# Projections two chunks at a time, latent statistics and key rope moved, attention's products in another order, in a two-layer hybrid decoder trunk on one NeuronCore

## The chip, the core and the metric

The kernel runs on one core of a Trainium2 chip. The metric is the device time of one execution in microseconds (us). TensorE (PE) multiplies, VectorE (DVE) and ScalarE (ACT) do the element-wise work, SyncE (SP) issues nearly all DMAs. TensorE writes to eight PSUM banks of 128 x 512 fp32.

## The reference

```python
# x: 256 tokens x 2048; layer 0: short convolution, layer 1: latent attention; both with a squared-ReLU MLP
bcu = h @ w_in                                   # 2048 -> 6144
gate_b, gate_c, u = split(bcu, 3)
mix = (gate_b * causal_conv3(gate_c * u)) @ w_out
h = LN(ALPHA * h + mix)
h = LN(ALPHA * h + square(relu(h @ w1)) @ w2)    # 2048 -> 8192 -> 2048
# layer 1
ckv = h @ w_dkv                                  # 512 latents and 64 for the key rope
c, k_pe = rms_norm(ckv[:, :512]) , rope(ckv[:, 512:])
k, v = split_heads(c @ w_ukv)                    # 16 heads, 128 each
q, q_pe = split_heads(rms_norm(h @ w_dq) @ w_uq) # 128 and 64 a head
p = softmax(mask((q @ k.T + rope(q_pe) @ k_pe.T) * 192 ** -0.5))
mix = (p @ v) @ w_o
h = LN(ALPHA * h + mix)
h = LN(ALPHA * h + square(relu(h @ w1)) @ w2)
```

## The kernel before

All products keep fp32 accuracy with a faster format: each fp32 operand is split into a high part (`hi`, ScalarE's cast) and a low part (`lo`, VectorE's subtraction). Activations stand transposed, high and low side by side in 512 columns, so a weight tile's high part meets 512 columns and its low part 256.

Weights come as units of 128 x 1024 (two for a chunk of 128 output columns from 2048 inputs). `stream` lists them in order of use; `take(n)` hands out the next n and has `make_up_to` load and split further ones ahead. The ring of finished parts has `WA = 8` slots, that of raw loads `RAW = 6`. Tiles in PSUM come from `psum`: four banks (`pmm`), and four more while `Banks` is open, which is so except in attention and in the parallel stretches of the MLP.

The order of the instructions on each engine is that of the code, changed by the framework's scheduler where dependencies allow; in the MLPs a planner (`Work`) writes it out.

The stages: an opening that multiplies while the first rows arrive, the input projection (`products(3 * NC, xhl, begun)`, 48 chunks in the order c, u, b, with the convolution between), the output projection (`products(NC, z)`, 16 chunks, name `ps_u` in both), the first MLP, the latents, attention, its output projection (three chunks in `out_first`, named `ps_wo`, then `products(NC - WO_G, oT)`, 13), the second MLP.

`mm_like` multiplies one chunk: 16 matmuls on high parts, then 16 on low parts. `products` takes a chunk, multiplies it and yields its bank.

At the first MLP's end `down` adds the last partial products into four blocks of 512 outputs, and `turned(n)` transposes a block into four chunks of 128 outputs (names `turned`, `xres`), which `summed` adds to the residual, counts for the layer norm (`S`, `Q`) and multiplies by the gain for the next product (`xd`). The next products are the latents: `group_of(GROUP)` opens three chunks (`ps_g`), which `mm_wide` runs over the inputs that are there.

The latents are nine chunks (four for keys and values, one for the key rope, four for queries); from the fourth on they are named `ps_w`. `latent` normalises a chunk after the fact, splits it and adds its squares (`csq`, `qsq`). `rms` turns those into a factor by a matmul with a column (`rstat`) and a root on a few values: `rc` for keys and values, spread over a tile `rk` by `spread` (`rkp`), and `rq`, from which `query_scale` makes `sc` and `nsc`. `rope` takes a product by cosines and four or two products by sines of 32 rows each, and a sum.

Attention runs in groups of four heads. `project(g)` makes a group's keys (`ps_k`, cleared by VectorE with `rk`), queries (`ps_q`, cleared by ScalarE), values (`ps_v`, ScalarE) and query ropes (`ps_p`, VectorE's `rope`), and yields after each; between its yields stands one step of `attention(g - 1)`: scores `S`, softmax, transposes `tp`, and the product with the values `po`. Only the four banks of `pmm` are left for `project`; attention has four of its own.

Of the kernel before, what the change touches and what calls it, by code (L numbers as in the profile page):

```python
# [53 lines left out]
def trunk(ctx: ExitStack, tc: tile.TileContext, opening, xT, vecs, w_in, w_out, w_kv, w_q, w_uk, w_uv,  # L54
# [75 lines left out]
    stream += mlp_stream(0)  # L130
    stream += mlp_end(0) + halves(w_kv) + halves(w_q)
    for g in range(4):
        stream += halves(w_uk[g]) + halves(w_qn[g]) + halves(w_uv[g]) + halves(w_qp[g])
    stream += halves(w_o) + mlp_stream(1)
    stream += mlp_end(1)
    size = {"unit": 1, "plain": 2}
# [108 lines left out]
            high(ps, w, k, x[k], k == 0)  # L245
            low(ps, w, k, x[k], k == nk - 1)

    def mm_like(ps, w, x, n=NC):

        for h in range(0, NC, n):  # L250
            for k in range(h, h + n):
                high(ps, w, k, x[k], k == 0)
            for k in range(h, h + n):
                low(ps, w, k, x[k], k == NC - 1)

    def mm_k1(ps, w, blk, x, first, last):
# [24 lines left out]
    def products(n, x, begun=()):  # L281

        yield from begun
        for i in range(len(begun), n):
            w = take()
            ps = psum("ps_u")
            mm_like(ps, w, x)
            yield ps


    def dot(ps, w, x, first, last, goes_on=False):
# [84 lines left out]
    class Norm:  # L376
# [10 lines left out]
        def means(self):  # L387

            ps = psum("mu0c")
            for t in range(2):  # L390
                tensor.matmul(ps[:, t:t + 1], xres[:, 0, t * P:(t + 1) * P], ones[:, 0:1], start=True, stop=True)
            self.off = small.tile([P, 2], F32, tag="off", name="off", bufs=1)
            vector.tensor_scalar(self.off, ps[:, 0:2], -self.scale, None, ALU.mult)

        def prepare(self, m):
# [690 lines left out]

    def to_wide(block, put, h):

        def turned(n):
            for c in range(2):  # L1090
                ps = psum("turned")
                for j in range(4):
                    src = block(n, j % 2)[:, (2 * c + j // 2) * P:(2 * c + j // 2 + 1) * P]
                    tensor.transpose(ps[:, j * P:(j + 1) * P], src, id_t)
                summed(ln, [ps[:, j * T:(j + 1) * T] for j in range(2)], scaled, 4 * n + 2 * c)

        ln.widen("b")
        for n in range(NB):
            down(h, put, n)
            if n:  # L1100
                turned(n - 1)
        ln.ws = group_of(GROUP)
        mm_wide(ln.ws, ln.xd, 0, NC - 4)
        turned(NB - 1)
        mm_wide(ln.ws, ln.xd, NC - 4)

    before, ln = ln, Norm(1, ALPHA)
# [6 lines left out]
    with tc.tile_pool(name="att", bufs=1) as ap:  # L1114
# [60 lines left out]
        pss = wide_products()  # L1175
        for m in range(NK):
            latent(next(pss), m, chl, C_KG, csq)
        f = tmp.tile([P, T], F32, tag="fh", name="fpe", bufs=3)
        ln.weighted(next(pss), f)
        for j in range(2):  # L1180
            rope(kpe[:, j, :], f, slice(64 * j, 64 * j + 64))
        for m in range(NK):
            ps = next(pss)
            if m == 0:
                rms(rc, csq)
            if m == 2:
                rkp = psum("rkp")
                spread(rkp, rc)
                scalar.copy(rk, rkp[:, :T])
            latent(ps, m, qhl, C_QG, qsq)  # L1190
        rq = small.tile([P, 2], F32, tag="rr", name="rq")

        def query_scale():
# [13 lines left out]
        with tc.tile_pool(name="att2", bufs=2) as a2, \  # L1207
                tc.tile_pool(name="paux", bufs=1, space=PS) as paux:
            def project(g, box):

                k4, q4, p4, v4 = (t[g % 2] for t in (k2, q2, p2, v2))
                box.update(k=k4, q=q4, p=p4, v=v4)
                w = take()
                for j in range(4):
                    ps = psum("ps_k")
                    mm(ps, w, 4 * j, chl, NK)
                    vector.tensor_tensor(k4[:, j, :], ps[:, :T], rk, ALU.mult)
                    yield
                w = take()
                for j in range(4):  # L1220
                    ps = psum("ps_q")
                    mm(ps, w, 4 * j, qhl, NK)
                    scalar.copy(q4[:, j, :], ps[:, :T])
                    yield
                if g == 0:
                    query_scale()
                for _ in range(2):
                    ln.normal(next(todo))
                w = take()
                for b in range(2):  # L1230
                    ps = psum("ps_v")
                    for k in range(NK):
                        dot(ps, wide_rows(w[k // 2], k % 2), held(chl[k], b), k == 0, k == NK - 1)
                    scalar.activation(v4[:, b, :], ps, AF.Copy, scale=rc[:, b:b + 1])
                    yield
                w = take(1)
                for j in range(2):
                    ps = psum("ps_p")
                    mm(ps, w, 4 * j, qhl, NK)
                    rope(p4[:, j, :], ps[:, :T], slice(0, P))  # L1240
                    yield

            def attend(h, box):

                j = h % 4
                qn, kn = box["q"][:, j, :], box["k"][:, j, :]
                qp, kp = box["p"][:, j // 2, :], kpe[:, h % 2, :]
                S = paux.tile([P, 512], F32, tag="S", name=f"S_{h}", bufs=2)
                spans = ((0, P), (P, T))
                for b, (at, n) in enumerate(spans):  # L1250
                    tok = slice(b * P, (b + 1) * P)
                    tensor.matmul(S[:, at:at + n], qn[:, tok], kn[:, :n], start=True, stop=False)
                    tensor.matmul(S[:, at:at + n], qp[:, tok], kp[:, :n], start=False, stop=True)
                pr = pr2[h % 2]
                mx = small.tile([P, 2], F32, tag="mx", name="mx")
                su = small.tile([P, 2], F32, tag="su", name="su")
                vector.tensor_tensor(pr, S[:, :3 * P], mask_t, ALU.add)
                for b, (at, n) in enumerate(spans):
                    vector.tensor_reduce(mx[:, b:b + 1], pr[:, at:at + n], AX.X, ALU.max)
                vector.tensor_tensor(mx, mx, nsc, ALU.mult)  # L1260
                for b, (at, n) in enumerate(spans):
                    scalar.activation(pr[:, at:at + n], pr[:, at:at + n], AF.Exp, bias=mx[:, b:b + 1],
                                         scale=sc[:, b:b + 1], accum_out=su[:, b:b + 1])
                vector.reciprocal(su, su)
                for b, (at, n) in enumerate(spans):
                    vector.tensor_scalar(pr[:, at:at + n], pr[:, at:at + n], su[:, b:b + 1], None, ALU.mult)
                yield
                tp = paux.tile([P, 512], F32, tag="ta", name="tp")
                for n in range(3):
                    tensor.transpose(tp[:, n * P:(n + 1) * P], pr[:, n * P:(n + 1) * P], id_t)  # L1270
                pt = a2.tile([P, 3 * P], F32, tag="pt", name=f"pt_{h}")
                scalar.copy(pt, tp[:, :3 * P])
                yield
                po = paux.tile([P, 512], F32, tag="tb", name="po")
                vv = box["v"]
                tensor.matmul(po[:, :T], vv[:, 0, j * P:(j + 1) * P], pt[:, :T], start=True, stop=False)
                tensor.matmul(po[:, P:T], vv[:, 1, j * P:(j + 1) * P], pt[:, T:], start=False, stop=True)
                put_split(oT[h], po[:, :T])
                yield

            def attention(g, box):
                gens = [attend(4 * g + j, box) for j in range(4)]
                for step in range(6):
                    for j in range(3, -1, -1):
                        if 0 <= step - j < 3:
                            next(gens[j])
                            yield

            first_o = []
            after = Norm(2, ALPHA)  # L1290

            def out_first():

                for i in range(WO_G):
                    first_o.append((take(), psum("ps_wo")))
                for k in range(H):
                    mm_run(first_o, oT, k, k + 1, H)
                    after.prepare(k)
                    yield

            prev = None
            for g in range(5):
                box = {}
                a = attention(g - 1, prev) if prev is not None else iter(())
                b = project(g, box) if g < 4 else out_first()
                done_a = done_b = False
                while not (done_a and done_b):
                    done_a = next(a, 0) == 0
                    done_b = next(b, 0) == 0
                prev = box  # L1310
# [143 lines left out]
```

## Time and profile before

| | us |
|---|---|
| median of 3 runs | 1997.64 |
| lowest and highest | 1997.62, 1998.24 |
| the profiled execution | 1998.73 |
| its span, first to last instruction | 1996.9 |

| stage, us from the span's start | PE busy | DVE busy | ACT busy |
|---|---|---|---|
| 100 to 150, input projection | 50.00 | 32.08 | 23.09 |
| 300 to 350, output projection | 50.00 | 39.04 | 25.31 |
| 500 to 600, first MLP | 100.00 | 95.97 | 85.50 |
| 1050 to 1100, latents | 48.62 | 44.71 | 34.73 |
| 1100 to 1150, latents and attention | 49.63 | 42.55 | 33.16 |
| 1250 to 1300, attention's output projection | 50.00 | 39.56 | 25.30 |

Nearly every instruction is recorded by one helper and so has line L71: groups are told apart by their names, `out<-in`. A row of the timeline has start, length, engine, line, operation, names, shape and count, and in square brackets the idle time before and what ended it. A matmul's end is modelled, and records of neighbours overlap: their pace is read from the starts.

### The profile page before, as it was taken

The numbers are of one execution on the slowest core, as the hardware profiler recorded it, in microseconds if no ns is written. First come the engines' busy times: TensorE is split into PE (matmuls) and PEld (weight loads), VectorE is DVE, ScalarE is ACT, GpSimd is POOL, SyncE is SP. The second block draws the span as 40 slices with busy tenths as digits, with TensorE's granted clock in tenths as the row PEclk, the third lists the DMA queues.
The fourth block names the chain that finished last, engine by engine and source line by source line (L and its number), as shares of the span: only waits on it lengthen the run. The fifth ranks groups of instructions, "written<-read, shape, count | busy, mean of one in ns | idle before, by whom it ended". The sixth has DMA issues, their size and how long they took to land.

```text
span 1996.9 us, 29770 instructions
## 1 busy us (share of the span) xinstructions
PE 1983.1 (99%) x11058; PEld 1735.0 (87%) x11058; DVE 1752.6 (88%) x2630; ACT 1388.6 (70%) x2069; POOL 2.3 (0%) x21
## 2 busy tenths in 40 slices
PE   9999999999999999999999999999999999999997
PEld 8888888988888888888889998898888888888886
DVE  7667667689999999999988888878999999999997
ACT  6444445577887888878856655567788788887871
POOL 0000000000000000000000000000000000000000
PEclk9999999999999999999999999999999999999999
DMA  9755556456666666666765543644666666666673
GB/s 341 230 188 189 191 186 188 156 164 195 208 200 202 205 202 205 200 202 207 221 208 158 165 129 117 204 163 154 201 203 206 200 203 204 202 206 202 199 248 110
DMA packets 107858, 387.39 MB, mean 194 GB/s; under 512 B 11969, under 2 KB 12737, under 8 KB 107713
## 3 DMA queue, kind: packets, MB, share of 16 engines
q1 hardware_dynamic: 107568, 385.36, 61.5%
q8 instruction: 86, 1.41, 0.3%
q14 instruction: 60, 0.48, 0.1%
q10 hardware_dynamic: 144, 0.13, 0.0%
HBM read 383.35 MB, written 2.10 MB: 193 GB/s over the span
## 4 chain that ended last, share of the span: by engine, by line
PE 98%; DVE 1%; issue 0%; ACT 0%; DVEq 0%
PE ps_m L71 31%; PE sum L71 27%; PE ps_u L71 20%; PE ps_d L71 4%; PE ps_w L71 4%; PE ps_g L71 4%; PE ps_q L71 1%; PE ps_v L71 1%; PE S L71 1%; PE ps_k L71 1%; PE ps_wo L71 1%; PE po L71 1%; PE ps_p L71 1%; PE turned L71 0%; DVE lo L71 0%
## 5 line engine op out<-in xcount | busy, mean ns | idle before, releaser
L71 DVE TENSOR_TENSOR lo<-w,hi 128x1024 fp32r<-128x1024 f32 x536 | 640.8, 1220 | 38.5 <-ACT hi L71 37.7
L71 ACT CAST hi<-w 128x1024 fp32r<-128x1024 f32 x536 | 541.8, 1061 | 64.2 <-DVE w L71 63.3
L71 ACT CAST hi<-raw 128x1024 fp32r<-128x1024 f32 x278 | 289.9, 1051 | 252.9 <-PE ps_u L71 155.0
L71 DVE TENSOR_TENSOR lo<-raw,hi 128x1024 fp32r<-128x1024 f32 x278 | 333.8, 1221 | 112.3 <-ACT hi L71 39.7
L71 PE MATMUL ps_m<-xhl,hi 128*128 128x512 f32 x1792 | 425.6, 390 | 0.0
L71 PEld LDWEIGHTS ps_m<-xhl,hi 128*128 128x128 f32 x1792 | 336.1, 188 | 71.7
L71 PE MATMUL sum<-hi,hc 128*128 128x512 f32 x736 | 278.0, 391 | 0.0
L71 PE MATMUL sum<-lo,hc 128*128 128x512 f32 x656 | 257.3, 392 | 0.0
L71 PE MATMUL sum<-hi,ha 128*128 128x512 f32 x640 | 246.5, 389 | 0.0
L71 PEld LDWEIGHTS ps_m<-xhl,lo 128*128 128x128 f32 x1792 | 229.8, 191 | 8.7
L71 PE MATMUL ps_m<-xhl,lo 128*128 128x256 f32 x1792 | 232.5, 283 | 0.0
L71 DVE TENSOR_TENSOR w<-w,w 128x512 f32<-128x512 f32 x312 | 213.7, 685 | 0.3
L71 PE MATMUL ps_u<-xhl_a,hi 128*128 128x512 f32 x704 | 168.1, 391 | 0.0
L71 PEld LDWEIGHTS sum<-hi,hc 128*128 128x128 f32 x736 | 138.6, 188 | 26.7 <-DVE t L71 0.3
L71 PEld LDWEIGHTS ps_u<-xhl_a,hi 128*128 128x128 f32 x704 | 129.4, 188 | 25.1
L71 PEld LDWEIGHTS sum<-hi,ha 128*128 128x128 f32 x640 | 120.2, 188 | 26.2
L71 PEld LDWEIGHTS sum<-lo,hc 128*128 128x128 f32 x656 | 123.6, 188 | 22.3
L71 ACT COPY sums<-sum 128x512 f32<-128x512 f32 x194 | 112.8, 596 | 12.3 <-PE sum L71 11.8
L71 ACT COPY t<-ps_m 128x256 f32<-128x256 f32 x112 | 42.4, 378 | 97.9 <-PE ps_m L71 97.9
L71 ACT COPY sum<-sums 128x512 f32<-128x512 f32 x174 | 105.4, 606 | 0.8
L71 PE MATMUL ps_w<-xd,hi 128*128 128x258 f32 x512 | 94.4, 284 | 0.5 <-DVE xres L71 0.5
L71 PEld LDWEIGHTS ps_u<-xhl_a,lo 128*128 128x128 f32 x704 | 90.3, 191 | 3.4
(201 smaller groups left out, 2785.4 us busy)
## 6 DMA issues: line engine op xcount, KB each, us to landing
w<-in_w_dram SPq DMA_DIRECT2D x224, 512.0 KB, 3.8
w<-in_w2f_dram SPq DMA_DIRECT2D x208, 512.0 KB, 4.3
raw<-in_w_in_dram SPq DMA_DIRECT2D x88, 512.0 KB, 4.5
raw<-in_w_dram SPq DMA_DIRECT2D x64, 512.0 KB, 4.4
raw<-in_w_out_dram SPq DMA_DIRECT2D x32, 512.0 KB, 4.2
raw<-in_w_o_dram SPq DMA_DIRECT2D x32, 512.0 KB, 3.7
raw<-in_w2f_dram SPq DMA_DIRECT2D x16, 512.0 KB, 4.6
row<-in_opening_dram SPq DMA_DIRECT2D x15, 384.0 KB, 5.0
```

Source lines behind the costliest of these rows:

```text
L71: ins = op(*args, **named)
```

## The change

```diff
@@ stream
-        stream += halves(w_uk[g]) + halves(w_qn[g]) + halves(w_uv[g]) + halves(w_qp[g])
+        stream += halves(w_uk[g]) + halves(w_uv[g]) + halves(w_qp[g]) + halves(w_qn[g])
@@ mm_like
-    def mm_like(ps, w, x, n=NC):
-        for h in range(0, NC, n):
-            for k in range(h, h + n):
+    def mm_like(units, x):
+        for w, ps in units:
+            for k in range(NC):
                 high(ps, w, k, x[k], k == 0)
-            for k in range(h, h + n):
+        for w, ps in units:
+            for k in range(NC):
                 low(ps, w, k, x[k], k == NC - 1)
@@ products
-        for i in range(len(begun), n):
-            w = take()
-            ps = psum("ps_u")
-            mm_like(ps, w, x)
-            yield ps
+        i = len(begun)
+        while i < n:
+            units = [(take(), psum("ps_u")) for _ in range(2 if i < n - 2 else 1)]
+            i += len(units)
+            mm_like(units, x)
+            for _, ps in units:
+                yield ps
@@ Norm.means
-            self.off = small.tile([P, 2], F32, tag="off", name="off", bufs=1)
+            self.off = small.tile([P, 2], F32, tag="nm", name="off")
@@ to_wide
-        def turned(n):
-            for c in range(2):
+        def turned(n, *cs):
+            for c in cs or range(2):
...
-        mm_wide(ln.ws, ln.xd, 0, NC - 4)
-        turned(NB - 1)
+        mm_wide(ln.ws, ln.xd, 0, NC - 8)
+        turned(NB - 1, 0)
+        mm_wide(ln.ws, ln.xd, NC - 8, NC - 4)
+        turned(NB - 1, 1)
         mm_wide(ln.ws, ln.xd, NC - 4)
@@ latents
-        f = tmp.tile([P, T], F32, tag="fh", name="fpe", bufs=3)
+        f = ap.tile([P, T], F32, name="fpe")
         ln.weighted(next(pss), f)
-        for j in range(2):
-            rope(kpe[:, j, :], f, slice(64 * j, 64 * j + 64))
         for m in range(NK):
             ps = next(pss)
-            if m == 0:
+            if m == 1:
                 rms(rc, csq)
-            if m == 2:
+            if m == 3:
                 rkp = psum("rkp")
                 spread(rkp, rc)
                 scalar.copy(rk, rkp[:, :T])
             latent(ps, m, qhl, C_QG, qsq)
+            if 0 < m < 3:
+                j = m - 1
+                rope(kpe[:, j, :], f, slice(64 * j, 64 * j + 64))
@@ project: the block of queries (ps_q, query_scale, two ln.normal) goes from behind the keys to behind the ropes
```

In the three projections TensorE takes two chunks together, the last one or two of a projection alone. Its order in the input projection, where `hi_388` and `hi_394` are the second chunk's high parts and `lo_377` and `lo_383` the first one's low parts:

```order
 L71 MATMUL ps_u<-xhl_a_100,hi_376 128x512 x8
 L71 MATMUL ps_u<-xhl_a_101,hi_382 128x512 x8
+L71 MATMUL ps_u<-xhl_a_100,hi_388 128x512 x8
+L71 MATMUL ps_u<-xhl_a_101,hi_394 128x512 x8
 L71 MATMUL ps_u<-xhl_a_100,lo_377 128x256 x8
 L71 MATMUL ps_u<-xhl_a_101,lo_383 128x256 x8
-L71 MATMUL ps_u<-xhl_a_100,hi_388 128x512 x8
-L71 MATMUL ps_u<-xhl_a_101,hi_394 128x512 x8
 L71 MATMUL ps_u<-xhl_a_100,lo_389 128x256 x8
 L71 MATMUL ps_u<-xhl_a_101,lo_395 128x256 x8
```

The second chunk's high parts move ahead of the first one's low parts; no matmul is added or left out.

At the end of the latents VectorE clears the key products. Before, its order there was this (`lat` and `qsq` are the last query latent, `t` and `nu` the normalisation of chunks):

```order
L71 TENSOR_TENSOR nu<-nu,ab_9713 128x256
L71 SCALAR_TENSOR_TENSOR t<-ab_9713,wgb,t 128x256
L71 TENSOR_TENSOR lo_10260<-raw_10257,hi_10259 128x1024
L71 TENSOR_TENSOR lo_10266<-raw_10263,hi_10265 128x1024
L71 SCALAR_TENSOR_TENSOR lat<-lat,vec 128x256
L71 TENSOR_TENSOR qsq<-qsq,sq 128x256
L71 TENSOR_TENSOR kqva_10246<-ps_k,rk 128x256 x4
```

and now it is this:

```order
L71 TENSOR_TENSOR kpe<-ropea,ropeb 64x256
L71 TENSOR_TENSOR nu<-nu,ab_9713 128x256
L71 TENSOR_TENSOR t<-ps_w,ab_9713 128x256
L71 TENSOR_TENSOR lo_10260<-raw_10257,hi_10259 128x1024
L71 SCALAR_TENSOR_TENSOR t<-ab_9713,wgb,t 128x256
L71 TENSOR_TENSOR lo_10266<-raw_10263,hi_10265 128x1024
L71 TENSOR_TENSOR kqva_10246<-ps_k,rk 128x256 x2
L71 SCALAR_TENSOR_TENSOR lat<-lat,vec 128x256
L71 TENSOR_TENSOR qsq<-qsq,sq 128x256
L71 TENSOR_TENSOR kqva_10246<-ps_k,rk 128x256 x2
```

Two of the four clearings (`kqva` from `ps_k`) come ahead of the last latent's two operations, and the key rope's last sum (`kpe`), which stood far ahead, now stands six rows before the first clearing.

Where attention's first head begins, VectorE now makes the query scale (from `rve` to `nsc`) between the operations of the first softmax (mask and maxima, `mx`):

```order
L71 TENSOR_SCALAR rve<-rstat 128x2
L71 TENSOR_TENSOR nu<-xres,ab_9713 128x256
L71 RECIPROCAL iv<-rve 128x2
L71 TENSOR_TENSOR kqva_10247<-S_10505,mask_t 128x384
L71 TENSOR_TENSOR rt<-sq,iv 128x2
L71 TENSOR_TENSOR lo_10530<-raw_10527,hi_10529 128x1024
L71 SCALAR_TENSOR_TENSOR ra<-sq,rt 128x2
L71 TENSOR_REDUCE mx<-kqva_10247 128x1
L71 SCALAR_TENSOR_TENSOR rq<-ra,rt 128x2
L71 TENSOR_REDUCE mx<-kqva_10247 128x1
L71 TENSOR_SCALAR sc<-rq 128x2
L71 TENSOR_SCALAR nsc<-rq 128x2
```

Before, `rve` to `nsc` stood ahead of the values and ropes of the first group, and no softmax operation was among them. On TensorE, from the later groups' first scores to the first transposes, 24 key products, 2 further products and two more sets of scores stood before; now 27 products and one set of scores do.

More of the change, by code (lines that the diff above doesn't have):

```diff
@@ L1219, in project @@
                 w = take()
[L1220 to L1229, printed above, removed]
                 for b in range(2):
@@ L1241, in project @@
                     yield
+                w = take()
+                for j in range(4):
+                    ps = psum("ps_q")
+                    mm(ps, w, 4 * j, qhl, NK)
+                    scalar.copy(q4[:, j, :], ps[:, :T])
+                    yield
+                if g == 0:
+                    query_scale()
+                for _ in range(2):
+                    ln.normal(next(todo))
             def attend(h, box):
```

## The prediction

> **What bounds the kernel now.** I read the page first, then the waits of TensorE, then the stages that the change touches, then single stretches of them in the timeline and the chain.
>
> ```profile
> span 1996.9 us, 29770 instructions
> PE 1983.1 (99%) x11058; PEld 1735.0 (87%) x11058; DVE 1752.6 (88%) x2630; ACT 1388.6 (70%) x2069; POOL 2.3 (0%) x21
> PEclk9999999999999999999999999999999999999999
> ```
>
> TensorE (PE) is busy for 1983.1 of 1996.9 us and its clock is granted nearly whole throughout. Only 13.8 us are idle, so no reordering can save more than that, unless it makes the matmuls themselves follow each other faster. The waits of TensorE say how little is the scheduler's to win:
>
> ```profile
> PE warm L71 <- DVE col L71: 1.1, 1, 1.1
> PE rstat L71 <- DVE csq L71: 0.8, 1, 0.8
> PE ps_w L71 <- DVE xres L71: 0.5, 1, 0.5
> PE S L71 <- DVE kqva L71: 0.4, 1, 0.4
> PE lnAB L71 <- DVE rr L71: 0.2, 1, 0.2
> ```
>
> Three of these five lie where the change works. The stages (us; busy us of each engine, its instructions in brackets, clock, DMA share, GB/s):
>
> ```profile
> 1041.00:1055.00 14.00, 14.00 (x119) 14.00 (x118) 11.17 (x22) 7.03 (x12) 0.00 (x0) 1.00 0.45 149
> 1055.00:1111.00 56.00, 54.62 (x451) 53.95 (x450) 52.21 (x116) 39.32 (x80) 0.00 (x0) 1.00 0.57 178
> 1111.00:1235.00 124.00, 123.63 (x815) 112.81 (x814) 98.77 (x251) 71.16 (x156) 0.00 (x0) 1.00 0.41 125
> 1235.00:1308.00 73.00, 73.00 (x422) 64.54 (x421) 60.67 (x102) 40.68 (x59) 0.00 (x0) 1.00 0.62 195
> 1940.00:1997.00 57.00, 46.05 (x215) 38.20 (x213) 41.81 (x66) 10.73 (x13) 0.00 (x0) 0.94 0.39 139
> ```
>
> From the end of the first MLP to the end of attention (1041 to 1235) TensorE idles 1.38 + 0.37 = 1.75 us. Of the 13.8 us the end of the kernel holds 57 - 46.05 = 10.95, which the change leaves alone. The third busy column is VectorE (DVE): with 52.21 of 56 us in the latent stage it is nearly as full as TensorE, and that is where a new wait could come from.
>
> **Part 1, projections two chunks at a time.** Nothing is added: the same matmuls stand in another order, highs of both chunks and then lows of both. Does a change between a run of highs and a run of lows cost anything?
>
> ```profile
> 95.52 3.82 PE L71 MATMUL ps_u<-xhl_a,hi 128*128 128x512 f32 x16
> 99.17 2.08 PE L71 MATMUL ps_u<-xhl_a,lo 128*128 128x256 f32 x16
> 101.09 3.82 PE L71 MATMUL ps_u<-xhl_a,hi 128*128 128x512 f32 x16
> 1093.13 5.76 PE ps_w L71 x48
> ```
>
> A run of sixteen highs takes 99.17 - 95.52 = 3.65 us (228 ns each), one of sixteen lows 101.09 - 99.17 = 1.92 (120 ns each). The chain's last row is a run of 48 matmuls of nearly the low's width, each with a new weight: 5.76 / 48 = 120 ns again. Sixteen lows between two runs of highs thus go at the pace of an endless run. The change from one to the other costs nothing, and halving the number of changes saves nothing: 0 us for the 34 pairs (21 in the input projection, 7 and 6 in the two output projections).
>
> What it can cost is lead. The second chunk's high weights are now wanted after one run of highs, not after a whole chunk: 5.57 - 3.65 = 1.92 us earlier. The lead is shortest at the opening:
>
> ```profile
> 29.08 1.06 ACT L71 CAST hi<-raw 128x1024 fp32r<-128x1024 f32 x1
> 30.55 2.98 ACT L71 CAST hi<-raw 128x1024 fp32r<-128x1024 f32 x3
> 28.70 3.84 PE L71 MATMUL ps_u<-xhl_a,hi 128*128 128x512 f32 x16
> 34.29 1.09 PE L71 MATMUL ps_u<-xhl_a,hi 128*128 128x512 f32 x4
> ```
>
> The first pair starts at 28.70. Its second chunk's first half is ready at 29.08 + 1.06 = 30.14 and the second half at about 31.6 (the first third of the row at 30.55). They were wanted from 34.29, and are now from 32.37 and 34.2: 2.2 us to spare. Later the eight-slot ring is full all the time, since a conversion starts as soon as a slot is free, and a pair holds half of it: the other half is two chunks, 11.1 us ahead. The copies to clear the two accumulators come 3.65 us later for the first chunk, with eight banks in use. 0 us, at the worst a one-time wait at the opening.
>
> **Part 2, the last block turned in two steps.** Here TensorE waits today:
>
> ```profile
> 1041.81 13.04 PE ps_g L71 x108
> 1056.23 0.36 PE L71 MATMUL ps_w<-xd,hi 128*128 128x258 f32 x1 [0.50 <-DVE xres L71]
> 1063.54 1.23 DVE lo L71
> 1064.82 2.79 PE ps_w L71 x21
> ```
>
> After the eight transposes nothing is ready: the chunk put in needs the bank that VectorE is clearing. Now the first four transposes come 4.3 us earlier (36 of the 108 matmuls that the chain has in 13.04 us), and the second four are followed by 18 matmuls on what the first four brought. The wait goes: 0.50. A second hold follows: the chain passes through a weight's low part (1063.54 + 1.23 = 1064.77, and the matmul that needs it starts at 1064.82). VectorE now has half of the work 4.3 us earlier, so this should go too. It is too short to be a row of the waits; its bounds are 0 and 0.2, the shortest wait listed, and I take 0.
>
> **Part 3, latent statistics one chunk later, key rope two.** The matmul of the statistics (rstat) waits 0.8 us for the last sum of squares. One chunk later, 5.76 us, that sum is long there: 0.82 goes. What is late next is what hangs on it: rc is needed by the transposes in front of the keys, and these move one chunk back as well, so their distance stays. The rope's eight VectorE operations leave the place in front of rstat's and go behind two later chunks:
>
> ```profile
> 1083.49 0.41 DVE L71 TENSOR_TENSOR ropea<-fpe,cos_t 64x256 f32<-64x256 f32 x1
> 1086.99 0.42 DVE L71 TENSOR_TENSOR kpe<-ropea,ropeb 64x256 f32<-64x256 f32 x1
> 1098.90 5.75 PE ps_k L71 x48
> 1103.93 1.42 DVE L71 TENSOR_TENSOR kqva<-ps_k,rk 128x256 f32<-128x256 f32 x4
> 1104.65 5.77 PE ps_q L71 x48
> ```
>
> They fill 1083.49 to 1087.41, with one other inside: about 3.4 us, closer now to the keys. VectorE is behind there: the first key product ends at 1098.90 + 5.75 / 4 = 1100.34 and is cleared at 1103.93 + 0.42 = 1104.35, 0.30 before TensorE wants that bank again (four banks in this stage). But the sum of work in front of the clearing is the same, and two of the clearings now stand ahead of the last latent's two operations in VectorE's order. Both engines come earlier by about the same. I take 0, and 0 to 1 us (the backlog of 4.0 worked off a quarter more slowly, an estimate) as bounds.
>
> **Part 4, attention's order keys, values, ropes, queries.** Queries are cleared by ScalarE (ACT), ropes by VectorE in six operations, and it was the last rope that the first scores waited for: 0.37 goes, since the ropes now have four query products after them. In exchange the query scale, once four products ahead of the first scores, now stands right before them. From its matmul to the first head's turned weights TensorE has three groups of scores (1.31 us for two) and 36 key products (1.44 for twelve): 6.3 us. VectorE and ScalarE need:
>
> ```profile
> L71 DVE TENSOR_SCALAR rve<-rstat x2: 151/155/159, 1082.7 to 1110.8; 128x2 f32<-128x2 f32 x2
> 1126.43 1.28 ACT L71 ACT_TABLE_LOAD   x1
> 1127.73 0.49 ACT L71 ACTIVATE kqva<-kqva,mx,sc 128x128 f32<-128x128 f32 x1
> L71 DVE TENSOR_TENSOR kqva<-S,mask_t 128x384 f32<-128x384 f32 x4 | 2.2, 546 | 0.0
> L71 DVE TENSOR_REDUCE mx<-kqva 128x1 f32<-128x256 f32 x4 | 1.6, 406 | 0.0
> L71 DVE TENSOR_SCALAR kqva<-kqva,su 128x256 f32<-128x256 f32 x4 | 1.4, 348 | 0.0
> L71 ACT ACTIVATE kqva<-kqva,mx,sc 128x256 f32<-128x256 f32 x4 | 2.4, 589 | 0.0
> 1126.76 1.31 PE S L71 x8
> 1128.07 1.43 PE ps_k L71 x12
> ```
>
> By these rows one softmax is 0.55 (mask), at most 2 x 0.41 (maxima), 2 x 0.59 (exponentials) and 2 x 0.35 (scalings): 3.25, and with an estimated 0.45 for its small operations 3.7 us. The scale is six small VectorE operations of 0.155 and a root on ScalarE, 1.1, with one low part of 1.23 between them in VectorE's new order: 2.3. Mask and maxima run between them, so the whole is 3.7 + 2.3 less up to 1.4: 4.6 to 6.0, just covered. The table row is what could break that, for ScalarE loads the exponential's table right behind the root; 1.28 us fit beside VectorE's maxima. In the trace the first exponential starts at the load's end.
>
> For the three later groups the cover shrinks. From the first scores' end to the first transpose there were 26 key and query products and some 1.2 us of scores (4.3 us); now there are 27 and 0.65: 3.9, against 3.7 and the hand-overs. Bounds 0 and 0.5 us for each group; I take 0.2, so 0.6 in all.
>
> **The sum.** Gone: 0.82 + 0.50 + 0.37 = 1.69. A run's last record reaches beyond the start of what follows (3.82 against 3.65 above: 0.17), so a gap is seen that much too short: three times 0.17, 0.5 more, 2.2. Added: 0.6. That is 1.6 us. The profiled execution took 1998.73 (its span 1996.9 and 1.8 around it), so it becomes 1997.1; the median shown is 1997.64, 1.1 less, and becomes 1996.0.
>
> **The rivals.**
> - *The gain is given back.* VectorE at 52.21 of 56 us may simply be the second bound: what TensorE no longer waits for at rstat it waits for at the keys or at the turned weights. With the upper bounds (1 + 3 x 0.5) the sum is +0.3: 1997.9. For it: 0.30 us of margin at the keys. Against: VectorE idles too in that stage (3.8 us), so it is not the bound throughout.
> - *Slower: rope in front of the keys.* If VectorE is late by the rope's 3.4 us when the keys' banks fill, TensorE stands 3.4 - 0.3 = 3.1 us before its fifth product. It decides once VectorE's backlog, 1104.35 - 1100.34 = 4.0 us today, passes 4.3. Then 1996.0 + 3.1 = 1999.1. Against: the four clearings come sooner in its order.
> - *The table is late.* If the load of 1.28 us cannot run beside VectorE's maxima, the first head needs up to 6.0 + 1.3 = 7.3 us against 6.3, and 1.0 of the gain is lost: 1997.0. Against: the trace's load ends 0.02 before the first exponential starts, with nothing behind it. The Trainium skill would have it so ("ScalarE: Activation LUTs", What ACT_TABLE_LOAD costs): a change of table set is there a load of about 1.28 us and a drain of 1.38 on top. The load agrees with the row; no drain stands in the trace.
> - *Slower: long runs of lows.* If the 16 highs' slack is what feeds the loads of the lows, a run of 32 could fall to the load's own time. The records of a load are 187 to 192 ns against the pace of 120, so 34 pairs x 16 x 0.07 = 38 us: 2034. The run of 48 at 120 ns speaks against it.
>
> ```profile
> L71 PEld LDWEIGHTS ps_u<-xhl_a,lo x704: 187/192/192, 32.2 to 273.8; 128*128 128x128 f32 x176
> ```
>
> The Trainium skill has a rule from which this would follow ("TensorE: Matmul & The Clock Gate", Back-to-back issue gap): the spacing of matmuls is set by load and matmul together, pipelined through a window of 64. The trace's run of 48 agrees with a pipeline that never falls behind.
>
> - *Faster by over 4 us.* It needs a faster pace of the matmuls, for which no row speaks.
>
> **How the numbers follow.** The forecast 0.65, given back 0.18, rope in front of the keys 0.07, a late table 0.05, long runs 0.02, faster by over 4 us 0.03. The low end takes all named waits, the 0.2 of part 2 and no new one (2.4), and up to 1 us of small waits in attention that records hide: 1994.2. The high end takes the gain given back and half of the second rival: 1998.4. A fifth of a per cent, 4 us, is about what a measurement of this kernel can tell from no change; all my cases but the last two lie within it. With 0.01 more above and 0.03 more below for what no row shows, faster has 0.04, same 0.91, slower 0.05.
>
> **What would show it.** Right: no wait of rstat on csq, none of ps_w on xres, none of S on the rope; runs of 32 highs and 32 lows at 228 and 120 ns; small waits of tp on VectorE or ScalarE in attention. Wrong: a wait of ps_v or ps_k for a bank, lows slower than 120 ns, or TensorE waiting for hi or lo in a projection.

## The result and the profile after

The changed kernel takes 1992.42 us (median of 8 runs, 1991.92 to 1992.99), the kernel before 1998.15 (median of its 8 runs beside it): a ratio of 0.9972, 95% interval 0.9963 to 0.9981. That is 5.7 us less, where 1.6 were forecast, and below the range.

The page of the profiled execution after (the span, the engines' busy time, TensorE's clock):

```profile
span 1991.1 us, 29733 instructions
PE 1978.0 (99%) x11058; PEld 1734.7 (87%) x11058; DVE 1742.3 (88%) x2630; ACT 1390.7 (70%) x2069; POOL 2.3 (0%) x21
PEclk9999999999999999999999999999999999999999
```

The span is 5.8 shorter, but TensorE's idle time has hardly moved: 1991.1 - 1978.0 = 13.1 against 13.8. What fell is its busy time, by 5.1, with the same 11058 matmuls. So most of the gain isn't a wait that went: matmuls follow each other faster, the one way in which the prediction said more than 4 us could go. The waits of TensorE after:

```profile
PE warm L71 <- DVE col L71: 1.1, 1, 1.1
PE ps_v L71 <- DVE kqva L71: 0.2, 1, 0.2
PE tp L71 <- DVE kqva L71: 0.2, 1, 0.2
```

All waits that the change was to remove are gone, and two small new ones stand where the prediction put them (a bank behind the keys, the transposes). The stages, in the same stretches and columns as before:

```profile
1055.00:1111.00 56.00, 55.76 (x444) 54.53 (x443) 52.36 (x112) 40.71 (x78) 0.00 (x0) 1.00 0.55 174
1111.00:1235.00 124.00, 123.06 (x817) 112.16 (x817) 100.37 (x253) 73.05 (x158) 0.00 (x0) 1.00 0.39 120
```

In the latents TensorE idles 0.24 instead of 1.38, in attention 0.94 instead of 0.37: 0.6 us won. The rest lies elsewhere. Matched matmul by matmul, the changed kernel's lead is 0.7 us where the first MLP's second product sets in and 2.9 at its end; over the second MLP it grows from 3.6 to 5.8. That is 4.4 us in code whose matmuls stand as before. Inside the MLP, the tile `t4` (in the rows `t`) is read as the 512 moving columns of three matmuls in each of 104 groups. The tile's view from 505 to 985 us (duration in ns: least, median, most; then the first and the last start), first before, then after:

```profile
L71 PE MATMUL sum<-t,hc x92: 393/396/399, 510.0 to 977.1; 128*128 128x512 f32 x92
L71 PE MATMUL sum<-t,ha x46: 397/397/398, 510.5 to 977.3; 128*128 128x512 f32 x46
```

```profile
L71 PE MATMUL sum<-t,hc x92: 389/389/389, 509.0 to 974.2; 128*128 128x512 f32 x92
L71 PE MATMUL sum<-t,ha x46: 388/389/389, 509.5 to 974.5; 128*128 128x512 f32 x46
```

The same 46 groups span 467.1 us before and 465.2 after, 1.9/45 = 42 ns a group, times 104: 4.4 us. No wait is listed there, and the order is the same. One thing differs: the line `self.off = small.tile(..., tag="nm", ...)` lets a tile of 8 bytes share a slot instead of having one of its own, and everything allocated behind it lies 32 bytes lower. `t4` moved from 224928 to 224896. These are the byte addresses that the build gives the tile in a partition's memory; those of the hi and lo parts, `hc`, `ha` and `xhl` all differ from 224896 by multiples of 512.

### The profile page after: what moved, and what is told of

Its sections match the earlier page's. It is cut to its first block, busy times and chain, and to the rows that moved or that the text cites. A ratio compares the mean times of both kernels' runs of the same rounds, so it can differ in the third digit from the quotient of the medians.

```text
span 1991.1 us, 29733 instructions
## 1 busy us (share of the span) xinstructions
PE 1978.0 (99%) x11058; PEld 1734.7 (87%) x11058; DVE 1742.3 (88%) x2630; ACT 1390.7 (70%) x2069; POOL 2.3 (0%) x21
## 4 chain that ended last, share of the span: by engine, by line
PE 95%; DVE 4%; issue 0%; ACT 0%; DVEq 0%; ACTq 0%
PE ps_m L71 31%; PE sum L71 27%; PE ps_u L71 20%; PE ps_d L71 4%; PE ps_g L71 4%; PE ps_w L71 3%; DVE lo L71 1%; PE ps_wo L71 1%; PE ps_v L71 1%; DVE ropeb L71 1%; PE S L71 1%; PE po L71 0%; DVE nu L71 0%; DVE kqva L71 0%; PE turned L71 0%
## 5 line engine op out<-in xcount | busy, mean ns | idle before, releaser
L71 PE MATMUL ps_u<-xhl_a,hi 128*128 128x512 f32 x704 | 164.1, 390 | 0.0
L71 ACT ACTIVATE sf<-sf 128x512 f32<-128x512 f32 x120 | 76.5, 637 | 27.3 <-DVE sf L71 27.2
```

Source lines behind the costliest of these rows:

```text
L71: ins = op(*args, **named)
```

## The experiments

Ratios are to runs of the kernel before beside them (medians 1997.8 to 1998.1).

**The tag alone, and undone.**

```diff
-            self.off = small.tile([P, 2], F32, tag="off", name="off", bufs=1)
+            self.off = small.tile([P, 2], F32, tag="nm", name="off")
```

> The kernel before with one line of the change alone: the small tile off takes a slot of the tag nm instead of one of its own, so that every tile allocated behind it, the MLP's t4 among them, lies 32 bytes lower (t4 at 224896, a multiple of 64, instead of 224928). Theory A (place of t4: 512-column matmuls that read t4 are slower from the old place): the 2 x 2.1 us by which the two traces differ inside the MLPs come with this line alone, so 4.2 us less, about 1994. Theory B (the gain comes from the reordering, which leaves the engines in another phase for the MLPs): no change, within 0.5 us of before.

> The changed kernel with that line alone undone (off has its own slot, t4 back at 224928). Theory A: 4.2 us more than the changed kernel, about 1996.6, so only 1.5 us under before, which is what the four reorderings give together. Theory B: as the changed kernel, about 1992.4.

The line alone: 1993.57 against 1997.98, ratio 0.9978 (0.9969 to 0.9987), 4.4 us less. Without it: 1996.75, 0.9995 (0.9986 to 1.0004). A holds, B falls: the line brings some three quarters of the gain, the four reorderings together 1.2 us.

**The place of t4.** In the kernel before, a further slot behind `off`; in the changed one, `t4` moved within a larger tile:

```diff
+            pad = small.tile([P, 2], F32, tag="pad", name="pad", bufs=1)
+            vector.memset(pad, 0.0)
```
```diff
-    box["f"] = fast.tile([P, 2, BW], F32R, tag="t4", name="t4", bufs=1)
+    box["f"] = fast.tile([P, 2 * BW + 8], F32R, tag="t4", name="t4", bufs=1)[:, 8:].rearrange(
+        "p (v c) -> p v c", v=2)
```

> The kernel before with off in its own slot and a further small tile of one slot behind it, so that t4 lies 32 bytes higher, at 224960, again a multiple of 64. Theory A (address): 4.2 us less, as with the shared tag, about 1994. Theory C (sharing the slot is what matters, or that the tiles lie lower): no gain, 1998.

> The changed kernel with t4 alone moved: its tile is 32 bytes larger and is used from its 32nd byte on, at 224928; the pairs of squares sf and all else stay where the changed kernel has them. Theory A with t4 as the only cause: 4.2 us more than the changed kernel, 1996.6, and matmuls with t4 as their 512 columns at 236 ns instead of 227. Rival (it was sf, which moved with it): no change, 1992.4.

`t4` alone by 32: 1996.61, 4.2 more than the changed kernel, so `t4` is the cause, not `sf`. The pad: 2001.2, ratio 1.0016 (1.0007 to 1.0025), 3.2 slower than before: a multiple of 64 is no cure. The same view of the two, the moved `t4` first, the pad second:

```profile
L71 PE MATMUL sum<-t,hc x92: 393/396/399, 508.6 to 975.6; 128*128 128x512 f32 x92
```

```profile
L71 PE MATMUL sum<-t,hc x92: 397/397/398, 509.1 to 977.3; 128*128 128x512 f32 x92
```

The first is the row of before again, with 467.0 us; the second takes 468.2, 3.0 more than after.

**Eight places in one run.**

```diff
-    box["f"] = fast.tile([P, 2, BW], F32R, tag="t4", name="t4", bufs=1)
+    box["f"] = fast.tile([P, 2 * BW + 56], F32R, tag="t4", name="t4", bufs=1)[:, 8 * (i % 8):][:, :2 * BW].rearrange(
+        "p (v c) -> p v c", v=2)
```

> The changed kernel with the slot of t4 made 224 bytes larger, and each group of the MLP's second product using it from another byte on: 0, 32, 64, and so on to 224 behind 224896, which is a multiple of 128 but not of 256. So far a group (three matmuls that read t4) takes 0, 41 and 71 ns more at 0, 32 and 64. Theory A1 (the place within 128 bytes counts): 128 is as 0, 160 as 32, 192 as 64; with some 60 ns at 96, 13 groups at each of 8 places give 4.5 us more, about 1997. Theory A2 (the place towards the end of the memory counts): it grows on, by some 35 ns for each 32 bytes, to 250 at 224, 13 us more, about 2005. Theory A3 (within 64 bytes: 64 in the padded kernel was slow for another reason): 0, 64, 128 and 192 are free, 2.1 us more, 1994.5.

1995.43, 0.9987 (0.9978 to 0.9996): 3.0 more than the changed kernel. From the starts in the trace (the matmul ahead of a group to the fourteenth behind it, 3400 ns at 224896, medians of 12 to 14 groups) a group takes longer by:

| bytes behind 224896 | 0 | 32 | 64 | 96 | 128 | 160 | 192 | 224 |
|---|---|---|---|---|---|---|---|---|
| ns | 0 | 47 | 73 | 33 | 40 | 27 | 40 | 27 |

A1 falls (128 isn't as 0), A2 falls (it doesn't grow), A3 falls (64 is the dearest). Of these eight places only the first is free, the one that differs from the other operands by a multiple of 512.

**Another operand by 32 bytes.**

```diff
-        xt = array("b", F32R, f"xhl{idx}", NC, 2 * T)
+        xt = act.tile([P, ROOM["b"] // 4], F32R, tag="b", name=f"xhl{idx}")[:, 8:][:, :NC * 2 * T]
+        xt = xt.rearrange("p (k t) -> p k t", k=NC)
```

> The changed kernel with the MLP's transposed activations xhl moved by 32 bytes within their array (61600 instead of 61568): the 512 columns of 1792 matmuls on high parts of ps_m and the 256 of 1792 on low parts now start off a multiple of 128, as those of t4 did before. Theory A1 (any 512-column operand pays for its place, 13 to 14 ns each): 24 us more, 2016; with half of that for each of 256 columns 36 us, 2028. Theory A2 (only the end of the memory): no change, 1992.4.

2000.47, 1.0012 (1.0003 to 1.0021): 8.1 more, between the theories. Groups of TensorE by form, after and then this kernel:

```profile
L71 PE MATMUL ps_m<-xhl,hi 128*128 128x512 f32 x1792 | 424.6, 389 | 0.0
L71 PE MATMUL ps_m<-xhl,lo 128*128 128x256 f32 x1792 | 232.5, 283 | 0.0
```

```profile
L71 PE MATMUL ps_m<-xhl,hi 128*128 128x512 f32 x1792 | 436.7, 395 | 0.0
L71 PE MATMUL ps_m<-xhl,lo 128*128 128x256 f32 x1792 | 229.3, 280 | 0.0
```

By the starts each of 1792 matmuls of 512 columns takes 6.7 ns longer (233.5 instead of 226.8; busy 12.1 us more), each of 256 columns 1.7 ns less (117.8 instead of 119.5). `xhl` lies far from the end of the memory, so the end isn't it. And within a run of sixteen all moving operands lie alike, yet every one pays: it isn't a change from one moving operand to the next.

**Everything moved, or the stationary operand alone.**

```diff
+    pad = const.tile([P, 8], F32, name="pad")      # 32 bytes; 32 and 64 elements for 128 and 256
+    vector.memset(pad, 0.0)
```
```diff
-        two = array("a2", F32R, f"ha{idx}", 4, 8 * P)
+        two = act.tile([P, ROOM["a2"] // 4], F32R, tag="a2", name=f"ha{idx}")[:, 8:][:, :32 * P]   # 64: for 256
+        two = two.rearrange("p (a c) -> p a c", a=4)
```

> The changed kernel with a tile of 32 bytes put in front, so that every array, weights and activations and t4 alike, lies 32 bytes higher. Theory F1 (the place of the 512 columns by itself counts): about 5000 matmuls of 512 columns at 6.7 ns each, some 30 us more, 2022 or above. Theory F2 (only the place against the weights, or against the other operands before and after, counts): all of that is unchanged, 1992.4.

> The same with 128 bytes. Under F1 this tells whether 128 bytes are a period: 1992.4 if so, some 30 us more if not. Under F2 1992.4.

> The same with 256 bytes. Under F1 with a period of 256 1992.4, with one of 512 or more some 30 us more. Under F2 1992.4.

> The changed kernel with the low parts ha of the MLP's middle moved by 32 bytes within their array: these are the stationary 128 columns of 896 matmuls (a third of those of the second product), never the 512 moving ones. F1: no change, 1992.4. F2: some 5 to 14 ns for each or for each change of it, 4 to 12 us more.

> The changed kernel with ha, the stationary operand of 896 matmuls of the second products, moved by 256 bytes instead of 32. If operands only have to differ by a multiple of 256: 1992.4. If of 512: several us more, up to the 13 that 32 bytes cost.

All by 32, 128 and 256: 1992.16, 1992.13 and 1992.27, as the changed kernel. `ha` alone by 32: 2005.34, 1.0036 (1.0022 to 1.0051), 12.9 more. `ha` by 256: 1992.49. F1 falls, F2 holds: what counts is where the operands of the matmuls lie against each other. Moving `ha` by 256 bytes is free; for the other operands this wasn't tried. Groups by form of the two runs with `ha` moved, by 32 and then by 256:

```profile
L71 PE MATMUL sum<-lo,hc 128*128 128x512 f32 x656 | 259.4, 395 | 0.0
L71 PE MATMUL sum<-t,hc 128*128 128x512 f32 x216 | 67.5, 397 | 0.0
```

```profile
L71 PE MATMUL sum<-lo,hc 128*128 128x512 f32 x656 | 256.5, 391 | 0.0
L71 PE MATMUL sum<-t,hc 128*128 128x512 f32 x216 | 65.8, 389 | 0.0
```

These rows read `hc`, which wasn't moved; behind a `sum<-lo,hc`, and behind the second of two `sum<-t,hc`, stands the matmul that takes `ha` as its weights. By the starts this neighbour of an `ha` loses most: 5.8 ns for a `sum<-lo,hc`, 12.5 for the second `sum<-t,hc`. But the other two of a round of three lose some 3 ns each as well. So what is slowed most is a matmul beside whose columns weights from another place are loaded. That the two reads get into each other's way is an inference: no record shows the memory's ports. The Trainium skill speaks against it ("TensorE: Matmul & The Clock Gate", Step-by-step: what each phase is for): TensorE has two independent read ports, and loading the next weights doesn't take bandwidth from the running matmul. By that rule moving `ha` would have cost nothing; it cost 12.9 us, and the measurement decides.

**The four parts, each alone on the kernel before** (the hunks of the diff above: `mm_like` and `products`; `to_wide`; the latents; `project` and its stream).

> The kernel before with part 1 alone (projections by two chunks at a time; off keeps its slot, so t4 lies as before). The prediction's step: 0. Theory D (a change from lows to highs costs: in the trace before the first five of sixteen highs start 240, 235, 228, 233 and 231 ns apart, then 227; the first low 113 instead of 120; together some 25 ns for a pair of changes): 34 pairs of changes less, 0.85 us less, about 1997.2.

> The kernel before with part 2 alone, the last block turned in two steps. The prediction's step: the wait of ps_w on xres goes, 0.50 and up to 0.37 more, so 0.5 to 0.9 us less. Rival: it reappears at rstat, whose wait for csq grows from 0.8 to 1.3 and more, since VectorE has the same work: no change.

> The kernel before with part 3 alone, the latent statistics one chunk later and the key rope two. The prediction's step: the wait of rstat goes, 0.8 to 1.0 us less. Rival: VectorE is late at the keys instead, and a wait of ps_q or ps_k for a bank of 0.4 and more takes part of it: 0.4 to 0.6 less.

> The kernel before with part 4 alone, attention's order keys, values, ropes, queries. The prediction's step: S no longer waits for the rope (0.4 to 0.5 less), three groups with 0.2 more each: within 0.2 of before. Theory E (the trace after shows starts late by 0.2 to 0.4 us at tp and po, four or five of them a group): 0.4 to 0.8 us more.

| part alone | median | against before, 1998.10 | forecast |
|---|---|---|---|
| pairs | 1997.26 | -0.84 | 0 |
| two steps | 1997.00 | -1.10 | -0.50 to -0.87 |
| statistics, key rope | 1997.58 | -0.52 | -0.82 to -0.99 |
| attention's order | 1998.66 | +0.56 | about 0 |

Each interval reaches over 1 (0.9987 to 1.0005 for the pairs, 0.9985 to 1.0003 for the two steps, 0.9988 to 1.0006 for the statistics, 0.9994 to 1.0012 for the order), so the medians only point. The traces agree with them: with the pairs alone TensorE's lead over the kernel before, taken matmul by matmul, grows by 0.7 us from the opening to the first MLP; from the end of that MLP to the end of attention it grows by 1.2 with the two steps, by 0.6 with the statistics, and falls by 0.5 with the order. The waits of TensorE with the two steps alone, and with the statistics alone:

```profile
PE rstat L71 <- DVE csq L71: 0.5, 1, 0.5
```

```profile
PE ps_q L71 <- DVE kqva L71: 0.7, 1, 0.7
```

The two steps shorten rstat's wait as well, from 0.8 to 0.5. Their 1.2 us of lead come in three places: 0.5 at the wait for `xres`, 0.3 at the second hold of the prediction (the starts from 1064.47 to 1065.04 take 0.58 before and 0.25 now), 0.4 at rstat. The statistics alone remove rstat's wait, which brings 1.1 us of lead, and meet the keys' bank with 0.7, where 0.9 of it goes again: the rival that gives the gain back. With all parts together a wait of 0.2 is left there, at the values, and 0.5 of lead goes.

**Runs of highs and lows.** The timeline of TensorE in the input projection, after:

```profile
95.39 7.44 PE L71 MATMUL ps_u<-xhl_a,hi 128*128 128x512 f32 x32
102.67 4.00 PE L71 MATMUL ps_u<-xhl_a,lo 128*128 128x256 f32 x32
106.50 7.44 PE L71 MATMUL ps_u<-xhl_a,hi 128*128 128x512 f32 x32
```

A pair takes 106.50 - 95.39 = 11.11, two chunks before took 2 x 5.57 = 11.14; in single starts the first five highs behind lows take 233, 236, 228, 233 and 231 ns (medians) and all others 227, and the first two lows 113 and 119 instead of 120: some 20 ns a change there and back. (The 240 of the expectation, from which its 25 ns follow, stands once among the 70 first highs of the trace before.) The opposite dose, on the kernel before:

```diff
-            mm_like(ps, w, x)
+            mm_like(ps, w, x, 4)
```

> The kernel before with its projections in runs of four highs and four lows instead of sixteen and sixteen: four pairs of changes for each of some 74 chunks instead of one, so 220 pairs more. The prediction's step (a change costs nothing): 1998. Theory D (25 ns a pair): 5.5 us more, 2003.5, somewhat less if four highs don't hold the whole of the five slow starts.

```profile
95.42 1.09 PE L71 MATMUL ps_u<-xhl_a,hi 128*128 128x512 f32 x4
96.35 0.63 PE L71 MATMUL ps_u<-xhl_a,lo 128*128 128x256 f32 x4
98.23 1.09 PE L71 MATMUL ps_u<-xhl_a,hi 128*128 128x512 f32 x4
```

2001.34, 1.0016 (1.0007 to 1.0026), 3.3 more: 15 ns for each of 3 x 73 further pairs of changes. By the rows two rounds of four take 98.23 - 95.42 = 2.81, a chunk 5.62 instead of 5.57. A change does cost.

**Attention's order.** The changed kernel with the old order, and with the query scale moved ahead of the ropes:

```diff
-        stream += halves(w_uk[g]) + halves(w_uv[g]) + halves(w_qp[g]) + halves(w_qn[g])
+        stream += halves(w_uk[g]) + halves(w_qn[g]) + halves(w_uv[g]) + halves(w_qp[g])
@@ project: the block of queries goes back to its place behind the keys
```
```diff
+                if g == 0:
+                    query_scale()
                 w = take(1)
                 for j in range(2):
                     ps = psum("ps_p")
...
-                if g == 0:
-                    query_scale()
```

> The changed kernel with part 4 undone (keys, queries, values, ropes as before), all else as changed. By the four parts alone the order costs 0.56: 1991.9, the best of all so far. Theory E': the order only costs alone and saves something beside the other parts: 1992.4 or more.

> The changed kernel with the query scale made behind the values, ahead of the ropes and the query products, two steps earlier; the order of the products stays. If the first head waits for the scale: the start of the first transposes, late by 0.4 in the trace, comes on time and the wait of tp goes, 0.4 us less, 1992.0. If the order costs in every group (the cover of 27 products and one set of scores is too short for a softmax): 1992.4, the late starts of the three later groups stay.

The old order takes 1991.4, 0.9966 (0.9954 to 0.9979): 1.0 less than the changed kernel and the lowest median of all. The two intervals overlap, but the traces agree: from the end of the first MLP to the end of attention TensorE's lead grows by 1.5 with the old order and by 0.6 with the new one. The early scale takes 1993.09, no gain; the wait of tp in the first head is 0.6 there, longer than the 0.2 of the changed kernel. The timeline of the changed kernel in a later group, VectorE and then TensorE:

```profile
1196.01 1.72 DVE L71 TENSOR_TENSOR ropeb<-ps_p,sin_t 32x256 f32<-32x256 f32 x4
1197.76 0.17 DVE L71 RECIPROCAL su<-su 128x2 f32<-128x2 f32 x1
1197.96 0.42 DVE L71 TENSOR_TENSOR ropea<-ps_p,cos_t 128x256 f32<-128x256 f32 x1
1198.30 0.54 DVE L71 TENSOR_SCALAR kqva<-kqva,su 128x128 f32<-128x128 f32 x2
```

```profile
1198.20 0.40 PE L71 MATMUL ps_q<-lat,hi 128*128 128x256 f32 x2
1198.72 0.61 PE L71 MATMUL tp<-id_t,kqva 128*128 128x128 f32 x3
```

Two matmuls of 120 ns stand between 1198.20 and the transposes, which would start at 1198.44; they start 0.28 late. What they wait for, the scaling at 1198.30, stood behind the ropes of the next group: VectorE's rope now falls into the softmax. With the scale early the same two rows stand at 1198.36 and 1198.88, just as late. With the old order no rope lies between:

```profile
1192.65 0.17 DVE L71 RECIPROCAL su<-su 128x2 f32<-128x2 f32 x1 [1.24 <-ACT kqva L71]
1192.85 0.55 DVE L71 TENSOR_SCALAR kqva<-kqva,su 128x128 f32<-128x128 f32 x2
```

## Why the prediction was wrong

The direction was right, the size wasn't, and the range missed. Three quarters of the gain came from a line that the prediction didn't price. By its steps:

- **The sum lacks a term.** The line with `off` was in the diff and had no place in the prediction: a tile of 8 bytes in another slot seemed to cost nothing and so wasn't costed. It moves `t4`, and that is 4.2 to 4.4 us by three runs (1993.57 with it alone; 1996.75 and 1996.61 without it). The four parts that were priced bring 1.2 to 1.4 together. That this lies near the sum of 1.6 is luck: alone they add up to 1.9, each of the four was off, and the errors of parts 1 and 2 offset those of parts 3 and 4.
- **"The change from one to the other costs nothing" was wrong.** It compared 120 ns of a run of lows with 120 of an endless one, but for the highs it had only 228 and nothing to hold beside it. An endless run of highs is at 227: by the starts 20 ns are lost at a pair of changes, 0.7 us for 34. The lead in the trace grew by as much up to the first MLP, and the median fell by 0.84.
- **Part 2 was too small**, 1.10 against 0.50 to 0.87: the second hold, bounded at 0.2 and taken at 0, was worth 0.3, and the same lead shortens rstat's wait too. **Part 3 was too large**, 0.52 against 0.82 to 0.99: alone it runs into the keys' bank, whose margin of 0.30 the prediction had read and priced at 0. With part 2 beside it, 0.5 of the lead still goes there, with a listed wait of 0.2.
- **Part 4 had the wrong sign.** The wait for the rope went. But the softmax was costed as an undisturbed chain of 3.7 us against a cover of 3.9, when VectorE's ropes had moved into it: by the medians 0.56 more alone, 1.0 in the changed kernel. The first head's scale, over which the prediction took most care, isn't the cause: made earlier, it saved nothing.
- **The rivals.** Given back in VectorE: true of most of part 3 alone, and of 0.5 us of lead with all parts together. Rope in front of the keys and a late table: no such wait in the trace. Long runs of lows: 106.50 - 102.67 = 3.83 for 32, 120 ns, so it fell. "Faster by over 4 us needs a faster pace, for which no row speaks" named the right quantity, but a row did speak: `sum<-t,hc` at 396 ns beside 389 for its neighbours of the same shape.

## What to carry to other kernels

Read a diff for what it does to the allocation as well as to the order: a small tile that comes or goes moves all that is allocated behind it. Compare the durations of matmuls of one shape across their operands; here a group that was 7 ns longer than its neighbours without any wait lay at another place. Places of the moving and the stationary operands that differ by a multiple of 512 bytes took 4 us off here; shifting one operand out of this by 32 bytes added 8 and 13 us, and a shift of 256, tried with `ha` alone, added none. And when a step moves between the steps of a chain on a shared engine, cost the chain with that engine's new queue, not with the sum of its own operations.

## What the runs showed of the hardware that was not expected

- A matmul's pace depends on where its 512 moving columns lie against the weights: 32 bytes off cost 6.7 ns each in an unbroken run (`xhl`, 226.8 to 233.5), and 32 to 224 bytes cost 27 to 73 ns for a group of three among others (`t4`); moving everything together by 32, 128 or 256 bytes costs nothing (1992.1 to 1992.3 us). For 256 columns the shift of 32 bytes made it 1.7 ns shorter (119.5 to 117.8). Why the eight places differ as they do stays open.
- Behind a run of 256-column matmuls the first five of 512 columns take up to 9 ns longer each (236 against 227), and some 20 ns are lost with a change there and back, 15 for each further pair when the runs are of four. Its cause stays open too.
